# Where the sums of the last MLP's weight blocks are made: in SBUF at the time of use, or in DRAM during the first layer

## The chip, the cores and the metric

The kernel runs on one core of one Trainium2 chip. The metric is the device time of one execution in microseconds (us); three runs of the kernel before took 2469.17, 2469.54 and 2475.82 us, with a median of 2469.54 us. One more execution was profiled, and all rows below come from it.

## The reference

Two transformer-like layers are applied to 640 tokens: 128 context tokens and 512 latent tokens, which share all weights. All tensors are float32, with D_MODEL 1024 and D_FF 2816.

```python
def _layer(x, mod, p, lam_init, ctx_kv, rope):
    sh1, sc1, g1, sh2, sc2, g2 = jnp.split(mod, 6, axis=-1)
    h = _rmsnorm(x, p['norm1']) * (1 + sc1) + sh1
    ...   # three mixers on h @ p['w_in']: two attentions and a pooling mixer -> oa, ob, oc
    ga, gb, gc = jnp.split(jax.nn.sigmoid(h @ p['w_gate'] + p['b_gate']), 3, axis=-1)
    merged = ga * (oa @ p['w_br_a']) + gb * (ob @ p['w_br_b']) + gc * (oc @ p['w_br_c'])
    x = x + g1 * (merged @ p['w_out'])
    h2 = _rmsnorm(x, p['norm2']) * (1 + sc2) + sh2
    a, g = jnp.split(_dwconv3(h2 @ p['w_up'], p['conv_w'], p['conv_b']), 2, axis=-1)
    x = x + g2 * ((jax.nn.silu(a) * g) @ p['w_down'])
    return x, own_kv
```

`mod` is `silu(cond) @ w_mod + b_mod`, with `w_mod` of 1024 x 6144 for each layer. The change concerns `h2 @ p['w_up']` of the second (last) layer.

## The kernel before

Activations lie transposed: 128 channels on the partitions, 640 tokens in the free dimension. Every product keeps float32 accuracy by splitting both operands into a high and a low float32r part (`split`, L96 to L98: ScalarE copies the high part, VectorE subtracts for the low part) and running three matmuls (`mm3`, L115 to L117). A weight tile is 128 x 1024 floats: `load_w` (L100) takes a staging buffer `st` (3 of them), has SyncE (SP) issue the load (L104), and splits it into `wh` and `wl` (5 of each).

A layer runs through an attention phase, a merge phase (gates and branch projections, `merge_phase`), an output projection (`out_phase`) and the MLP. In the first layer the MLP goes through `mlp_up` (L860): 22 tile pairs f, each with one 128-channel tile of the part a and one of the part g; 48 matmuls go over each tile. Four groups of tile pairs (6, 6, 5, 5) are each followed by their share of the down projection (8 tiles each). `mod_steps` (L131) runs beside merge and MLP: it loads `w_mod` tiles of 512 KB and reduces them on VectorE. Its loads are paced (`paced`, L125): GpSimd (POOL) first copies one column from a tile that the compute has just made into the buffer, so that SP must wait for it.

The last layer's MLP (`mlp_last`, L1058) does the first three tile pairs in the plain way (`plain`, L916) and the other 19 with seven block products in place of eight (`SevenUp`). The weights of a tile pair are four blocks of 128 x 512, A(r, c), with r the part (a or g) and c the half of the 1024 inputs; the tokens are two halves of 320. The seven products need three plain blocks (`a11`, `a12`, `a22`) and four sums of blocks (`s1`, `s3`, `s2`, `s4`, with 2, 2, 3 and 4 terms). The token-side sums `n1`, `t2`, `n3`, `n4` are made once (`tokens`, L947). A call of `step` (L996) begins tile pair f and finishes the one before it, so the products of two pairs are interleaved; each product (`prod`, L991) is 12 matmuls. The three PSUM banks of a pair (`oa`, `od`, `ob`) are read by ScalarE and VectorE into `ua` and `ug` between the products (L1026 to L1048), and then go through the convolution and the gate (`conv`, `gated`).

`weights` (L969) loads two blocks into one tile. A sum is made in the staging buffer itself: SP loads its first term (L981), and POOL issues one accumulating DMA for every further term:

```python
                for m in range(1, 4):
                    for at, up in parts:
                        if m < len(up):
                            pool.dma_start(at, up[m], accum_op=ALU.add)
```

Each of these waits until the transfer before it into the same bytes has landed. Only then is the tile split and used. There are 133 loads and 133 accumulating transfers of 256 KB.

The order of instructions on each engine is set when the program is built, by a planner that simulates the program with its own costs and places instructions by priority; on the chip each engine, and each engine's DMA queue, runs its list in order. SP issues all plain DMAs in one list, POOL the accumulating ones between its other work.

Of the kernel before, what the change touches and what calls it, by code (L numbers as in the profile page):

```python
# [12 lines left out]
F32 = mybir.dt.float32  # L13
# [7 lines left out]
P = 128  # L21
# [5 lines left out]
L = 2  # L27
F_T = 22
EPS = 1e-6
GROUPS = [(0, 6), (6, 12), (12, 17), (17, 22)]  # L30
PLAIN = 3
WINDOWS = (2, 4, 8, 16)
FILL = [[], [('u', 3), ('u', 2), ('u', 1)], [('u', 0), ('g', 16)], [('g', 17), ('g', 18), ('p', 3), ('p', 2)], [('g', 19), ('p', 1), ('p', 0)], [('g', 20), ('g', 8)], [('g', 9), ('g', 10)]]
REST = [('g', 11)]
# [23 lines left out]
def trunk_kernel(ctx: ExitStack, tc: tile.TileContext, a: dict):  # L58
# [33 lines left out]
    g_dram = dram.tile([24, P, T], F32, name="g_dram")  # L92
    cs_dram = dram.tile([1, 2, 1024], F32, name="cs_dram")
    x_dram = dram.tile([P, ND, T], F32, name="x_dram")

    def split(x, hi, lo, eng=vec):  # L96
        act.activation(hi, x, AF.Copy)  # L97
        eng.tensor_tensor(out=lo, in0=x, in1=hi.bitcast(F32), op=ALU.subtract)  # L98

    def load_w(src, cols, eng=vec, after=None):  # L100
        st = wp.tile([P, 1024], F32, tag="st", name="st", bufs=3)
        if after is not None:
            pool.tensor_copy(st[:, 0:1], after)
        dma(st[:, :cols], src)  # L104
        hi = wp.tile([P, 1024], F32R, tag="wh", name="wh")
        lo = wp.tile([P, 1024], F32R, tag="wl", name="wl")
        split(st[:, :cols], hi[:, :cols], lo[:, :cols], eng)
        return hi, lo
# [22 lines left out]
    def mod_steps(l, groups, rp, cs, nst=3, npr=1, on_pool=()):  # L131

        for g in groups:
            got = small.tile([P, 8, 2], F32, tag="got", name="got")
            for m in range(8):
                st = rp.tile([P, 1024], F32, tag="stm", name="stm", bufs=nst)
                paced(st, a["w_mod"][l, 8 * g + m])
                for j in range(2):
                    col = got[:, m, j:j + 1]
                    if j == 0 and m in on_pool:  # L140
                        pr = rp.tile([P, 1024], F32, tag="pr", name="pr", bufs=npr)
                        pool.tensor_tensor(out=pr, in0=st, in1=cs[:, j], op=ALU.mult)
                        act.activation(pr, pr, AF.Copy, accum_out=col)
                    else:
                        junk = rp.tile([P, 1024], mybir.dt.bfloat16, tag="junk", name="junk", bufs=1)
                        vec.scalar_tensor_tensor(out=junk, in0=st, scalar=1.0, in1=cs[:, j], op0=ALU.mult,  # L146
                                                 op1=ALU.mult, accum_out=col)
                if m == 7:
                    bm = vecs[l][:, V_BM + 8 * g:V_BM + 8 * g + 8].unsqueeze(2).to_broadcast([P, 8, 2])
                    vec.tensor_tensor(out=mods[l][:, 8 * g:8 * g + 8], in0=got, in1=bm, op=ALU.add)  # L150
                yield

    def scale_cols(l, vcol, sc, name):
        t = small.tile([P, 8, 2], F32, tag=name, name=name, bufs=1)
# [592 lines left out]
            for _ in chain(flush(), *(run(j) for j in range(at, len(stream)))):  # L747
                pass

    def merge_phase(l, x, cs, hh, hl, mp, ps_d, msteps):  # L750

        m32 = [None] * 8
        for bi, br in enumerate((2, 1, 0)):
            oh = [None] * 4
            ol = [None] * 4

            def operands():
                for k in range(4):
                    oh[k] = mp.tile([P, T], F32R, tag="oh", name="oh", bufs=4)
                    ol[k] = mp.tile([P, T], F32R, tag="ol", name="ol", bufs=4)  # L760
                    st = mp.tile([P, T], F32, tag="so", name="so", bufs=3)
                    dma(st, o_dram[4 * br + k])
                    split(st, oh[k], ol[k])

            def gate(n, early0=False):
                gt = mp.tile([P, T], F32, tag="gt", name="gt", bufs=4)
                if br * 8 + n in GATED:
                    dma(gt, g_dram[br * 8 + n])
                    act.activation(gt, gt, AF.Sigmoid)
                    return gt  # L770
                gh, gl = load_w(a["w_gate"][l, br * 8 + n], 1024)
                gp = ps_d.tile("gp", bi > 0 or not early0)
                for k in range(ND):
                    ks = slice(k * P, (k + 1) * P)
                    for c, (a0, b0) in enumerate(CH_B):
                        mm3(gp[:, c, :320], gh[:, ks], gl[:, ks], hh[:, k, a0:b0], hl[:, k, a0:b0],
                            k == 0, k == 7)
                act.activation(gt.rearrange("p (c n) -> p c n", c=2), gp[:, :, :320], AF.Sigmoid,
                               bias=vecs[l][:, V_BG + br * 8 + n:V_BG + br * 8 + n + 1])
                return gt  # L780

            order = list(range(7, -1, -1) if br == 2 else range(8))
            wb, gts = None, {}
            for i, n in enumerate(order):
                for m in order[i:i + (LOOK if br == 2 and i == 0 else 2)]:
                    if m not in gts:
                        gts[m] = gate(m, i == 0)
                gt = gts[n]
                gv = gt.rearrange("p (c n) -> p c n", c=2)
                if i % 2 == 0:  # L790
                    wb = load_w(a["w_br"][l, br, n // 2], 1024)
                if i == 0:
                    operands()
                bp = ps_d.tile("bp")
                for k in range(4):
                    ks = slice(((n % 2) * 4 + k) * P, ((n % 2) * 4 + k + 1) * P)
                    for c, (a0, b0) in enumerate(CH_B):
                        mm3(bp[:, c, :320], wb[0][:, ks], wb[1][:, ks], oh[k][:, a0:b0], ol[k][:, a0:b0],
                            k == 0, k == 3)
                after[0] = gt[:, 0:1]  # L800
                if bi > 0:
                    if bi == 1:
                        if n == 0:
                            paced(cs[:, 0], cs_dram[:, 0].to_broadcast([P, 1024]))
                            paced(cs[:, 1], cs_dram[:, 1].to_broadcast([P, 1024]))
                        paced(x[:, n], (a["x"] if l == 0 else x_dram)[:, n])
                    if bi == 1 or n < 4:
                        next(msteps, None)
                        next(msteps, None)
                if bi == 0:  # L810
                    m32[n] = mp.tile([P, T], F32, tag="m32", name="m32", bufs=8)
                    vec.tensor_tensor(out=m32[n].rearrange("p (c n) -> p c n", c=2), in0=bp[:, :, :320], in1=gv,  # L812
                                      op=ALU.mult)
                else:
                    vec.tensor_tensor(out=gv, in0=bp[:, :, :320], in1=gv, op=ALU.mult)
                    (pool if bi == 1 else vec).tensor_tensor(out=m32[n], in0=m32[n], in1=gt, op=ALU.add)
# [68 lines left out]
    class SevenUp:  # L885
# [6 lines left out]


        BUFS = 7
        SUMS = {"a11": ((0, 0),), "a12": ((0, 1),), "a22": ((1, 1),), "s1": ((1, 0), (1, 1)), "s3": ((1, 0), (0, 0)),
                "s2": ((1, 0), (0, 0), (1, 1)), "s4": ((0, 1), (1, 0), (0, 0), (1, 1))}

        def __init__(self, l, h2h, h2l, mp, ps):
            self.l, self.h2h, self.h2l, self.mp, self.ps = l, h2h, h2l, mp, ps
# [69 lines left out]
        def weights(self, blocks):  # L969

            w = {}
            for i in range(0, len(blocks), 2):
# [1 line left out]
                st = wp.tile([P, 1024], F32, tag="st", name="st", bufs=3)  # L974
                hi = wp.tile([P, 1024], F32R, tag="wh", name="wh")
                lo = wp.tile([P, 1024], F32R, tag="wl", name="wl")
                parts = []
                for k, (q, f) in enumerate(two):
                    up = [a["w_up"][self.l, r * F_T + f, :, 512 * c:512 * c + 512] for r, c in self.SUMS[q]]
                    parts.append((st[:, k * 512:(k + 1) * 512], up))  # L980
                    dma(parts[-1][0], up[0])  # L981
                    w[q, f] = hi[:, k * 512:(k + 1) * 512], lo[:, k * 512:(k + 1) * 512]
                for m in range(1, 4):
                    for at, up in parts:
                        if m < len(up):
                            pool.dma_start(at, up[m], accum_op=ALU.add)  # L986
                n = 512 * len(two)
                split(st[:, :n], hi[:, :n], lo[:, :n])
                yield w
# [193 lines left out]
    a0, b0 = CH_S[2]  # L1183
    modulate(rp, x, rstd0(a0, b0), A1, mods[0][:, 0:8], a0, b0, hh[:, :, a0:b0], hl[:, :, a0:b0])
    sst.close()
    for l in range(L):
        dst.close()
        rst.close()
# [10 lines left out]
        with ExitStack() as ms:  # L1199
            mp = tp("mg", 1, ms)  # L1200
            cs = modp.tile([P, 2, 1024], F32, tag="cs", name="cs", bufs=1)
            msteps = mod_steps(l, range(2, 6 if l + 1 < L else 5), modp, cs)
            m32 = merge_phase(l, x, cs, hh, hl, mp, ps_d, msteps)
            hst.close()
            hst = ExitStack()
            hp = tp("h2p", 1, hst, side="right")
# [9 lines left out]
        with ExitStack() as ms:  # L1216
# [4 lines left out]
            def up_to(f):  # L1221
                for i in range(len(ups), f):
                    ups[i] = mlp_up(l, i, h2h, h2l, mp, ps_d)
                    for _ in range(1 if i < GROUPS[0][1] + 2 else 2):
                        next(msteps, None)

            for gi, (f0, f1) in enumerate(GROUPS):
                up_to(min(F_T, f1 + 2))
# [150 lines left out]
```

## Time and profile before

| | |
|---|---|
| runs | 2469.17, 2469.54, 2475.82 us |
| profiled execution | 2470.33 us, span 2468.6 us, mean granted TensorE clock 0.958 |
| busy share of the span | TensorE (PE) 90%, weight load 88%, VectorE (DVE) 67%, ScalarE (ACT) 42%, POOL 26% |
| HBM | read 282.91 MB, written 22.95 MB |
| layer 1: merge and out / MLP | about 390 to 690 / 690 to 1175 us |
| layer 2: attention / merge and out / MLP | about 1175 to 1550 / 1550 to 1819 / 1819 to 2468.6 us |

The span is the time from the first to the last instruction. Times in rows are us from its start unless marked ns. Matmuls overlap: one of 320 columns shows a duration near 310 ns, while the spacing is read from how many fit into a stretch. A row of waits says which engine and line waited, for which work, how long in total, how often, and the longest. A row of windows gives the busy us (and instructions) of PE, PEld (weight load), DVE, ACT and POOL in that order, then the granted TensorE clock as a share of 2.4 GHz, the busy share of the 16 DMA engines, and GB/s. Queue q0 is POOL's, which before holds little but the accumulating DMAs; q1 is SP's. L12 is line 12 of the kernel.

### The profile page before, as it was taken

How to read it: one execution, taken by the hardware profiler on the slowest of the kernel's cores; microseconds unless marked ns; L12 is line 12 of the kernel's file. 1: busy time of each engine (PE TensorE's matmuls, PEld its weight loads, DVE VectorE, ACT ScalarE, POOL GpSimd, SP SyncE). 2: the span in 40 equal slices, each digit the busy share in tenths (PEclk: the TensorE clock that was granted, in tenths of full speed). 3: DMA queues.
4: the chain of work that ended last, by engine and by line, in shares of the span. 5: the costliest groups of instructions: out<-in, count | busy, mean ns of one | idle time of the engine just before them, and what ended most of it. 6: DMA issues, size and time to landing. Idle time of an engine off the chain costs nothing. (4 is left out here: it accounts for less than half of the span.)

```text
span 2468.6 us, 38189 instructions
## 1 busy us (share of the span) xinstructions
PE 2233.9 (90%) x14550; PEld 2167.6 (88%) x14550; DVE 1644.7 (67%) x2983; ACT 1029.4 (42%) x1868; POOL 647.7 (26%) x784
## 2 busy tenths in 40 slices
PE   8998999999999999999898999999997786596868
PEld 4998989999999999999798989999996786596867
DVE  7876786496677576767877686489567535435536
ACT  5454654422454242434455565422345413313333
POOL 4753331051310000002653433042222112112120
PEclk8999999999999999999999999999998898798989
DMA  7212223574433334335121222375336666666665
GB/s 254 76 40 65 78 91 101 183 265 146 128 96 99 105 129 128 117 119 156 54 72 55 84 82 89 130 283 186 108 95 136 147 134 141 138 131 141 137 133 145
DMA packets 135611, 308.36 MB, mean 125 GB/s; under 512 B 23170, under 2 KB 36226, under 8 KB 135427
## 3 DMA queue, kind: packets, MB, share of 16 engines
q1 hardware_dynamic: 116276, 271.04, 33.8%
q0 software_dynamic: 19152, 34.87, 9.1%
q8 instruction: 115, 1.88, 0.3%
q14 instruction: 68, 0.56, 0.1%
HBM read 282.91 MB, written 22.95 MB: 124 GB/s over the span
## 5 line engine op out<-in xcount | busy, mean ns | idle before, releaser
L98 DVE TENSOR_TENSOR wl<-st,wh 128x1024 fp32r<-128x1024 f32 (+3 forms) x374 | 410.0, 1103 | 288.8 <-ACT wh L97 288.2
L97 ACT ACTIVATE wh<-st 128x1024 fp32r<-128x1024 f32 (+3 forms) x374 | 343.7, 931 | 483.8 <-DMA st<-in_w_up 211.2
L146 DVE SCALAR_TENSOR_TENSOR junk<-stm,cs 128x1024 bf16<-128x1024 f32 x172 | 220.3, 1281 | 56.1 <-DMA stm<-in_w_mod 53.4
L986 POOL DMA_DIRECT2D st<-in_w_up x133 | 116.1, 941 | 478.6 <-DMA st<-in_w_up 337.6
L116 PE MATMUL up<-h2l,wh 128*128 128x320 f32 x704 | 218.2, 311 | 1.3 <-DVE h2l L212 1.2
L115 PE MATMUL up<-h2h,wl 128*128 128x320 f32 x704 | 217.1, 311 | 1.2 <-ACT v L874 0.7
L117 PE MATMUL up<-h2h,wh 128*128 128x320 f32 x704 | 217.8, 310 | 0.0
L115 PE MATMUL mm<-wh,hl 128*128 128x384 f32 x480 | 170.8, 356 | 14.3 <-ACT raw L364 10.6
L116 PE MATMUL mm<-wl,hh 128*128 128x384 f32 x480 | 164.9, 343 | 1.3 <-DVE wl L98 1.3
L117 PE MATMUL mm<-wh,hh 128*128 128x384 f32 x480 | 164.5, 343 | 0.0
L117 PE MATMUL gp<-hh,wh 128*128 128x320 f32 x480 | 148.6, 310 | 0.0
L115 PE MATMUL gp<-hh,wl 128*128 128x320 f32 x480 | 148.4, 309 | 0.0
L116 PE MATMUL gp<-hl,wh 128*128 128x320 f32 x480 | 148.3, 309 | 0.0
L115 PE MATMUL mmu<-hh,wl 128*128 128x384 f32 (+1 forms) x416 | 133.5, 321 | 4.0 <-ACT up L680 2.0
L116 PEld LDWEIGHTS up<-h2l,wh 128*128 128x128 f32 x704 | 132.8, 189 | 1.8 <-DVE h2l L212 1.8
L115 PEld LDWEIGHTS up<-h2h,wl 128*128 128x128 f32 x704 | 132.3, 189 | 2.0 <-ACT h2h L211 1.1
L117 PEld LDWEIGHTS up<-h2h,wh 128*128 128x128 f32 x704 | 132.7, 189 | 0.1
L117 PE MATMUL mmu<-hh,wh 128*128 128x384 f32 (+1 forms) x416 | 130.5, 314 | 0.0
L116 PE MATMUL mmu<-hl,wh 128*128 128x384 f32 (+1 forms) x416 | 129.9, 312 | 0.0
L128 POOL COPY stm<-v 128x1 f32<-128x1 f32 x32 | 24.6, 792 | 381.7 <-DVE v L879 328.1
L115 PE MATMUL bp<-oh,wl 128*128 128x320 f32 x384 | 117.6, 311 | 3.6 <-DVE m L812 1.8
L116 PE MATMUL bp<-ol,wh 128*128 128x320 f32 x384 | 118.7, 310 | 2.1 <-DVE ol L98 2.1
(321 smaller groups left out, 6897.7 us busy)
## 6 DMA issues: line engine op xcount, KB each, us to landing
stm<-in_w_mod SPq DMA_DIRECT2D x88, 512.0 KB, 4.2
st<-in_w_up SPq DMA_DIRECT2D x133, 256.0 KB, 3.8
st<-in_w_up POOLq DMA_DIRECT2D x133, 256.0 KB, 5.6
st<-in_w_up SPq DMA_DIRECT2D x50, 512.0 KB, 3.6
st<-in_w_gate SPq DMA_DIRECT2D x48, 512.0 KB, 3.8
st<-in_w_unit SPq DMA_DIRECT2D x48, 384.0 KB, 3.3
st<-in_w_out SPq DMA_DIRECT2D x32, 512.0 KB, 3.5
st<-in_w_down SPq DMA_DIRECT2D x48, 320.0 KB, 3.2
```

Of the source, the lines that this page charges most:

```text
L97: act.activation(hi, x, AF.Copy)
L98: eng.tensor_tensor(out=lo, in0=x, in1=hi.bitcast(F32), op=ALU.subtract)
L115: pe.matmul(out, sl, mh, start=start, stop=False, skip_group_check=parts)
L116: pe.matmul(out, sh, ml, start=False, stop=False, skip_group_check=parts)
L117: pe.matmul(out, sh, mh, start=False, stop=stop, skip_group_check=parts)
L128: pool.tensor_copy(dst[:, 0:1], after[0])
L146: vec.scalar_tensor_tensor(out=junk, in0=st, scalar=1.0, in1=cs[:, j], op0=ALU.mult, op1=ALU.mult, accum_out=col)
L986: pool.dma_start(at, up[m], accum_op=ALU.add)
```

## The change

The four sums of each of the 19 tile pairs are made once, in a DRAM buffer `s_dram`, while the first layer runs. `sum_steps` is a generator with 22 steps. In step i SP issues four DRAM to DRAM copies of 256 KB for pair i (queued behind the latest weight load on SP's list), and POOL issues up to four accumulating DRAM to DRAM transfers: two for pair i-1 (s1 and s3, from `w_up`), one for pair i-2 (s2, adding the finished s1) and one for pair i-3 (s4, adding the finished s2). The steps are taken after each third tile of the merge phase (two per branch, six in all) and after four of five tile pairs of the first layer's MLP. In the last MLP all seven blocks are then plain loads by SP; `weights` issues nothing on POOL.

```diff
+    s_dram = dram.tile([F_T, 4, P, 512], F32, name="s_dram")
...
-        dma(st[:, :cols], src)
+        loads[:] = [dma(st[:, :cols], src)]
...
+    def sum_steps(l):
+        def A(r, c, f):
+            return a["w_up"][l, r * F_T + f, :, 512 * c:512 * c + 512]
+
+        def add(f, k, src):
+            if PLAIN <= f < F_T:
+                pool.dma_start(s_dram[f, k], src(f), accum_op=ALU.add, max_dma_last_dim=512)
+
+        for i in range(PLAIN, F_T + 3):
+            if i < F_T:
+                with tc.issue_after(loads[-1].ins):
+                    for k, (r, c) in enumerate(((1, 0), (1, 0), (0, 0), (0, 1))):
+                        dma(s_dram[i, k], A(r, c, i))
+            add(i - 1, 0, lambda f: A(1, 1, f))
+            add(i - 1, 1, lambda f: A(0, 0, f))
+            add(i - 2, 2, lambda f: s_dram[f, 0])
+            add(i - 3, 3, lambda f: s_dram[f, 2])
+            yield
...
+                if i % 3 == 2:
+                    next(ssteps, None)
...
-                parts = []
                 for k, (q, f) in enumerate(two):
-                    up = [a["w_up"][self.l, r * F_T + f, :, 512 * c:512 * c + 512] for r, c in self.SUMS[q]]
-                    parts.append((st[:, k * 512:(k + 1) * 512], up))
-                    dma(parts[-1][0], up[0])
+                    if q in self.PLACE:
+                        r, c = self.PLACE[q]
+                        src = a["w_up"][self.l, r * F_T + f, :, 512 * c:512 * c + 512]
+                    else:
+                        src = s_dram[f, SUMS.index(q)]
+                    dma(st[:, k * 512:(k + 1) * 512], src)
...
-                for m in range(1, 4):
-                    for at, up in parts:
-                        if m < len(up):
-                            pool.dma_start(at, up[m], accum_op=ALU.add)
...
+                    if i % 5 != 4:
+                        next(ssteps, None)
```

## Rows read from the trace of the kernel before

**Rows 1.** Windows: length, busy us (instructions) of five engines; PEclk, DMA share, GB/s.
```profile
690.00:1127.00 437.00, 433.53 (x2937) 431.70 (x2936) 300.42 (x527) 160.60 (x214) 27.38 (x36) 1.00 0.35 111
...
1700.00:1750.00 50.00, 50.00 (x343) 50.00 (x342) 31.70 (x45) 11.90 (x13) 1.82 (x4) 1.00 0.37 126
...
1870.00:1895.00 25.00, 7.01 (x32) 5.95 (x30) 14.61 (x19) 7.04 (x12) 4.75 (x6) 0.70 0.52 102
1895.00:1970.00 75.00, 57.47 (x343) 56.69 (x344) 46.76 (x67) 32.36 (x52) 14.39 (x17) 0.83 0.63 137
1970.00:2020.00 50.00, 47.34 (x322) 46.94 (x321) 24.41 (x41) 13.45 (x19) 9.59 (x11) 1.00 0.64 148
2020.00:2140.00 120.00, 75.59 (x429) 73.13 (x427) 54.48 (x74) 40.32 (x67) 26.12 (x30) 0.84 0.66 136
2140.00:2190.00 50.00, 42.50 (x272) 42.50 (x273) 24.88 (x39) 14.58 (x20) 6.11 (x7) 0.87 0.56 139
2190.00:2300.00 110.00, 75.68 (x438) 73.61 (x436) 48.25 (x68) 35.28 (x58) 25.28 (x29) 0.86 0.65 134
2300.00:2345.00 45.00, 41.46 (x272) 41.46 (x273) 23.96 (x41) 13.95 (x20) 6.08 (x7) 0.92 0.59 141
2345.00:2425.00 80.00, 49.44 (x289) 47.87 (x288) 35.98 (x51) 27.57 (x45) 15.70 (x18) 0.82 0.61 126
2425.00:2469.00 44.00, 38.72 (x259) 38.20 (x257) 26.78 (x48) 14.33 (x22) 0.00 (x0) 0.97 0.52 161
```

**Rows 2.** Waits of PE, 1819 to 2469 us.
```profile
PE ob L115 <- DVE wl L98: 82.4, 10, 11.0
PE od L115 <- DVE ua L1044: 21.8, 4, 9.6
PE od L115 <- DVE wl L98: 18.7, 7, 7.3
```

**Rows 3.** Waits of DVE and of ACT, 1819 to 2469 us.
```profile
DVE wl L98 <- ACT wh L97: 222.1, 64, 12.1
...
ACT wh L97 <- DMA st<-in_w_up: 211.2, 31, 14.9
```

**Rows 4.** Line L986, the accumulating DMAs: issue (min/median/max ns) and time to landing.
```profile
L986 POOL DMA_DIRECT2D st<-in_w_up x133: 862/865/1575, 1823.3 to 2416.7; - x133
...
DMA to landing us min/median/max: 3.7/5.6/9.0
```

**Rows 5.** Timeline of DVE, 1866 to 1900 us: start, duration, instruction, idle before.
```profile
1878.46 1.22 DVE L98 TENSOR_TENSOR wl<-st,wh 128x1024 fp32r<-128x1024 f32 x1 [11.00 <-ACT wh L97]
...
1884.82 3.02 DVE L960 TENSOR_TENSOR f<-h2h,h2l 128x640 f32<-128x640 f32 x4
```

**Rows 6.** DMA issues (part 6 of the page): count, KB each, median us to landing.
```profile
st<-in_w_up SPq DMA_DIRECT2D x133, 256.0 KB, 3.8
...
st<-in_w_up SPq DMA_DIRECT2D x50, 512.0 KB, 3.6
...
g_dram<-z SPq DMA_DIRECT2D x18, 320.0 KB, 2.2
gt<-g_dram SPq DMA_DIRECT2D x18, 320.0 KB, 3.9
```

**Rows 7.** DMA queues: packets, MB, share of 16 engines' span.
```profile
q1 hardware_dynamic: 116276, 271.04, 33.8%
q0 software_dynamic: 19152, 34.87, 9.1%
```

**Rows 8.** Window in the merge phase of layer 1, columns as in rows 1.
```profile
500.00:525.00 25.00, 25.00 (x172) 25.00 (x172) 24.60 (x32) 6.35 (x7) 15.22 (x13) 1.00 0.75 270
```

**Rows 9.** Waits of SP's queue and of POOL, 390 to 1130 us.
```profile
SPq L104 <- DVE wl L98: 338.2, 72, 27.2
SPq L129 <- POOL stm L128: 139.9, 49, 6.7
...
POOL stm L128 <- DVE v L879: 328.1, 17, 54.9
```

More of the change, by code (lines that the diff above doesn't have):

```diff
@@ L31 @@
 PLAIN = 3
+SUMS = ("s1", "s3", "s2", "s4")
 WINDOWS = (2, 4, 8, 16)
@@ L98, in split @@
         eng.tensor_tensor(out=lo, in0=x, in1=hi.bitcast(F32), op=ALU.subtract)
+    loads = []
     def load_w(src, cols, eng=vec, after=None):
@@ L748, in attention_phase, with merge_phase @@
                 pass
-    def merge_phase(l, x, cs, hh, hl, mp, ps_d, msteps):
+    def merge_phase(l, x, cs, hh, hl, mp, ps_d, msteps, ssteps):
         m32 = [None] * 8
@@ L894, in trunk_kernel @@
         BUFS = 7
-        SUMS = {"a11": ((0, 0),), "a12": ((0, 1),), "a22": ((1, 1),), "s1": ((1, 0), (1, 1)), "s3": ((1, 0), (0, 0)),
-                "s2": ((1, 0), (0, 0), (1, 1)), "s4": ((0, 1), (1, 0), (0, 0), (1, 1))}
+        PLACE = {"a11": (0, 0), "a12": (0, 1), "a22": (1, 1)}
         def __init__(self, l, h2h, h2l, mp, ps):
@@ L1185, in trunk_kernel @@
     sst.close()
+    ssteps = sum_steps(L - 1)
     for l in range(L):
@@ L1202, in trunk_kernel @@
             msteps = mod_steps(l, range(2, 6 if l + 1 < L else 5), modp, cs)
-            m32 = merge_phase(l, x, cs, hh, hl, mp, ps_d, msteps)
+            m32 = merge_phase(l, x, cs, hh, hl, mp, ps_d, msteps, ssteps)
             hst.close()
```

## The prediction, made before the changed kernel ran

> **What bounds the kernel now.** I first read the windows, stage by stage. In the first layer's MLP PE is busy 433.5 of 437 us, so that stage is bound by PE and hides its loads; a comparable stretch of the second layer's output projection, which like the seven products uses a weight tile for only 24 matmuls, holds 343 matmuls in 50.00 us, or 145.8 ns each [rows 1]. The last MLP is another matter. It has 3 x 96 plain matmuls, 19 x 7 x 12 = 1596 of the products and 3 x 8 x 2 x (6 + 6 + 5) + 240 = 1056 of the down projection. The four stretches in which the products run take 75 + 120 + 110 + 80 = 385 us [rows 1]. About 24 of the product matmuls lie before 1895 us, so these stretches do 1572, which at 145.8 ns is 229 us. They lose 156 us: PE is busy 57.5 + 75.6 + 75.7 + 49.4 = 258 us of them, so 127 us is idle, and the rest (258 - 229 = 29) is the granted clock of 0.82 to 0.86: part of the time at 1.2 in place of 2.4 GHz.
>
> Second I read who ended these waits. PE waits mostly for `wl`, the low half of a split weight tile (82.4 + 18.7 us), and 21.8 us for a VectorE operation on a bank [rows 2]. VectorE waits 222.1 us for the high half, and ScalarE, which makes it, 211.2 us for the DMA of the weights [rows 3]; so the releaser of the chain is a transfer, and a bank that is read late is partly VectorE stuck behind such a tile. Third, the line that issues the transfers: an accumulating DMA takes 0.865 us on POOL and lands a median 5.6 us after its issue [rows 4], and a tile needs up to three in a row after a load of 3.8 us [rows 6]: 3.8 + 3 x (0.9 + 5.6) = 23 us with three staging buffers, where the products want a tile per 24 x 0.1458 = 3.5 us. The DMA engines are 61 to 66% busy there [rows 1], so it is latency in a chain, with bandwidth left over, that limits the stage.
>
> **What the change removes.** All 133 accumulating DMAs leave the last MLP, and with them the chain. A tile then arrives 3.8 us after its load; adding the split (1.22 us on VectorE [rows 5], and ScalarE's part taken as long) gives about 6.2 us, against 3 x 3.5 = 10.5 us that three buffers allow. So weights should be on time.
>
> (1) Start of the products. VectorE stands 11.0 us in its list, until 1878.46, for the first late tile, and begins the token sums only at 1884.82 [rows 5]. PE has 7.0 us of work in the 25 us from 1870 to 1895 [rows 1]. The token sums stay, and so does PE's wait for them; the 11.0 us goes, of which I count 10. The products would run from 1885 us.
>
> (2) The products. What is late next? VectorE's busy time in the four stretches is 46.8 + 54.5 + 48.3 + 36.0 = 185.5 us over 1572 / 84 = 18.7 pairs, or 9.9 us a pair; ScalarE's 135.5 us, or 7.2; PE's 84 x 0.1458 = 12.25 us [rows 1]. PE is the bound, VectorE is at 81% of it and in order, and bank reads must fall between products. Lower end: PE with 3% loss, 236 us. Upper end: 15.5 us a pair, 290 us, the pace of the first stretch after its start (75 us for about 4.7 pairs is 16 [rows 1]), where the sums were no less late. I take 10% over the pure matmul time, 252 us: nearer to the output projection's row, which has the same need of weights and no loss, than to today's pace. That is 385 - 252 = 133 us less.
>
> (3) The down projections. 1056 matmuls are 154 us and take 50 + 50 + 45 + 44 = 189 us today; their losses are the clock (0.87 and 0.92 in two of the four) and waits at the seams with the products. The first stretch, at clock 1.00, holds 322 matmuls in 50 us, 6.5% over the pure time [rows 1]. With that everywhere, 164 us, and 4 us for the last additions and store: 168 us. Ends 160 and 185.
>
> So the last MLP ends at 1885 + 252 + 168 = 2305 in place of 2468.6 us.
>
> **What it adds to the first layer.** 76 copies and 76 adds of 256 KB, DRAM to DRAM, a kind that this trace doesn't show. POOL: 76 x 0.865 = 66 us of issuing, at most four (3.5 us) at a step; POOL is busy 27.4 of 437 us in that MLP [rows 1] and spends 328.1 us waiting for a VectorE result before its pacing copies [rows 9]. DMA engines: SP's queue moved 271.04 MB in 33.8% of 2468.6 us, 325 GB/s while busy; POOL's 34.87 MB in 9.1%, 155 GB/s [rows 7]. The copies' 19.9 MB then take 61 us of engine time (128 at POOL's rate), the adds' 128 us; the lower bound for the adds is 61 us, the upper one is one transfer at a time, 76 x 5.6 = 426 us [rows 4]. In the MLP stretch 13 groups of copies and 59 adds fall, 42 + 100 us, beside 0.35 x 437 = 153 us of today's traffic [rows 1]: 295 of 437, a share of 0.68, which fits. In the merge phase the share is already 0.75 and VectorE is busy 24.6 of 25 us [rows 8]; a step adds about 3 + 7 = 10 us of engine time where some 6 of 25 us is free, so loads get late by some us at about three steps. SP normally waits for free buffers there (338.2 us [rows 9]), so loads run ahead, and most of this is hidden. I take 8 us of lost PE time in the first layer, with ends -3 (no row shows anything that could be gained but PE's idle 3.5 us) and +35 (adds at half of POOL's rate: 295 becomes 395 of 437, and every merge step late). The cover is the prefetch: three staged and five split tiles, each good for 48 matmuls or 7 us. SP's copies wait for nothing; POOL's adds wait for copies or adds of the step before, at least 14 us old (96 matmuls). Queued behind a waiting add are POOL's pacing copies, for which SP waits (139.9 us in 49 waits today, 6.7 at most [rows 9]), and behind them the weight loads.
>
> Span 2305 + 8 = 2313. The profiled execution took 2470.33 us for 2468.6 of span, 1.7 more, and stands 0.8 above the median of the runs: **2315 us**, 6.3% less.
>
> **Rivals.**
> A. The products stay late for another reason: VectorE's order, or a bank read that comes too late, takes the place of the transfers, and each stall costs some us at the 1.2 GHz level as now. For it: VectorE at 81% of PE's time, 21.8 us of PE's waits on `ua` [rows 2]. Against: VectorE itself waited 222.1 us for weights [rows 3]. At 15.5 us a pair and 180 us of down projections: 2315 + 38 + 12 = 2365.
> B. PE runs through, as in the output projection: products 236, downs 160 us, first layer nothing: 2315 - 16 - 8 - 8 = 2283, and 2275 if the tokens come earlier too.
> C. Slower than before: the adds saturate the DMA engines in the first layer, and the weight loads there get late, where PE has nothing to spare. For that the last MLP's 164 us must be lost again. 437 + 164 = 601 us of engine time, less 153 and 42, leaves 406 us for 59 adds (15.5 MB): the point is at 38 GB/s, a quarter of POOL's rate [rows 7]; at 35 GB/s the time would be 2507. Against: the two ends of an add are memory, and of the two single sides the trace shows that 320 KB written to DRAM lands in 2.2 us while the same read takes 3.9 [rows 6], so a write isn't the slow side. The Trainium skill ("DMA: Bandwidth & Descriptors", section on the anatomy of one DMA on the SWDGE path) says the opposite, that completion waits for the write's receipt and takes surprisingly long when the target is HBM; by it the adds would land later than 5.6 us and hold POOL's list, by the rows no later, and in either case the wait is for a transfer issued a step earlier. The same page (section "Issuing engines are not separate DMA queues") has POOL's and SP's transfers share the same engines; the trace agrees: beside the accumulates a 256 KB load takes 3.8 us, elsewhere 512 KB takes 3.6 [rows 6]. That is what keeps C alive.
> D. The change doesn't do what it says: reads of the sums wait for the adds, because the adds lag. The last step is taken in the MLP's pair 18 of 22, so before 1127 us [rows 1], and the first sums are read near 1820 [rows 4]; a lag of 700 us is out of reach. Under 1%, time as before.
>
> **Chances.** The forecast, 2285 to 2335: 55%. A, 2335 to 2400: 24%. B, below 2285: 14%. Between 2400 and 2460 (A and half of C together): 3%. C: 3%; D and other ways to no change: 1%. Leaving out about 2 in 10, the range is 2275 to 2380. A run can be told from no change at about 0.3% (7 us): faster 0.95, same 0.01, slower 0.04.
>
> **What the changed profile would show.** Waits of ScalarE for the DMA of `w_up` in the last MLP near 20 to 40 us in place of 211; no accumulating DMA after 1175 us, and POOL nearly idle there; token sums beginning within a few us of 1874; windows of products with 270 or more matmuls in 50 us and a clock over 0.95. In the first layer: PE still over 430 of 437 us, with a DMA share near 0.65; if it is 0.9 or over and PE has waits for `wl`, the engine-time sum is wrong and C's mechanism is at work. If adds land in over 15 us, POOL's rate doesn't hold between two places in memory. The prediction is wrong in its main step if the product stretches shrink by less than 90 us while the weights come on time; then it is VectorE's order that was under it.

## The result, and the profile after

The changed kernel took 2332.14 us (median of 4 runs, 2327.22 to 2334.83) against 2471.29 us for the kernel before in the same comparison; the ratio is 0.9432, with a 95% interval from 0.9409 to 0.9456. The prediction was 2315 us. Its profiled execution took 2327.22 us, with a span of 2325.4 us. The total hides two moves in opposite directions. The last output-projection matmul of the second layer, after which the last MLP runs, started at 1868.5 us where it had been at 1818.8; from there to the end it was 649.8 us before and is 456.9 now. So the last MLP gained 193 us, and all that comes ahead of it lost 50.

The last MLP first. Windows of the kernel after, columns as in [rows 1]: token sums, a stretch of products, the first down projection, the next products, and all from the first product with token sums on.
```profile
1915.00:1932.00 17.00, 7.47 (x51) 7.21 (x50) 12.95 (x17) 5.82 (x11) 0.00 (x0) 0.80 0.25 80
1932.00:1985.00 53.00, 51.37 (x332) 50.97 (x333) 48.17 (x69) 34.34 (x55) 0.00 (x0) 0.93 0.41 119
1985.00:2036.00 51.00, 51.00 (x350) 51.00 (x349) 27.94 (x45) 15.74 (x22) 0.00 (x0) 1.00 0.29 93
2036.00:2115.00 79.00, 79.00 (x540) 79.00 (x539) 66.75 (x95) 49.90 (x82) 0.00 (x0) 1.00 0.45 139
...
1932.00:2318.00 386.00, 382.88 (x2585) 381.99 (x2586) 283.47 (x425) 195.70 (x306) 0.00 (x0) 0.99 0.40 122
```
PE is busy 382.9 of 386 us at a granted clock of 0.99 (2.4 GHz nearly throughout). The second stretch of products, 429 matmuls in 120 us before [rows 1], now holds 540 in 79.00 us without a gap: 146.3 ns each, where the output projection's stretch had 145.8. (The bounds of the stretches are drawn by hand, so they don't hold the same matmuls.) The waits of [rows 2] and [rows 3], for the kernel after from 1819 to 2330 us, which takes in the 50 us ahead of the last MLP (PE, VectorE, ScalarE):
```profile
PE od L119 <- ACT n L99: 9.9, 1, 9.9
PE oa L119 <- DVE wl L100: 1.5, 1, 1.5
```
```profile
DVE wl L100 <- ACT wh L99: 40.8, 58, 5.1
```
```profile
ACT wh L99 <- PE ob L121: 66.9, 44, 4.7
...
ACT wh L99 <- DMA st<-in_w_down: 9.9, 5, 4.0
```
Here the direction has turned round: ScalarE's splits wait for PE to give buffers back, not for `w_up` to arrive: no wait for it is left. PE's one long wait is for the token sums.

Now the first layer. The same stretch as the first row of [rows 1], and the waits of POOL, SP, VectorE and PE from 390 to 1180 us:
```profile
690.00:1127.00 437.00, 401.94 (x2646) 397.59 (x2645) 282.09 (x494) 148.96 (x204) 81.19 (x86) 0.96 0.65 163
```
```profile
POOL s_dram L166 <- DMA s_dram<-in_w_up: 204.8, 32, 21.2
...
POOL s_dram L166 <- DMA s_dram<-s_dram: 80.1, 17, 8.5
```
```profile
SPq L133 <- POOL stm L132: 183.3, 42, 15.7
```
```profile
DVE junk L150 <- DMA stm<-in_w_mod: 97.5, 23, 12.2
```
```profile
PE up L119 <- ACT v L902: 17.4, 5, 7.7
```
The last two of these, in the kernel before:
```profile
DVE junk L146 <- DMA stm<-in_w_mod: 40.4, 20, 3.3
```
```profile
PE up L115 <- ACT v L874: 0.7, 1, 0.7
```
PE holds 291 matmuls fewer in the 437 us, which is 42 us of work at 145.8 ns: 31.6 us of busy time are gone, and the rest goes with a granted clock of 0.96 in place of 1.00. POOL stands 284.9 us in front of its adds (L166). The other three rows are the links by which that reaches PE. One instance can be followed in the timelines of the kernel after, POOL, SP, VectorE, ScalarE and PE, 800 to 830 us (start, duration, engine, instruction, idle time before it and its releaser):
```profile
801.88 1.06 POOL L166 DMA_DIRECT2D s_dram<-s_dram  x1 [3.69 <-DMA s_dram<-in_w_up]
807.39 1.01 POOL L166 DMA_DIRECT2D s_dram<-s_dram  x1 [4.46 <-DMA s_dram<-s_dram]
808.04 0.56 POOL L132 COPY stm<-v 128x1 f32<-128x1 f32 x1
```
```profile
808.62 0.33 SPq L133 DMA_DIRECT2D stm<-in_w_mod  x1
```
```profile
813.38 1.23 DVE L150 SCALAR_TENSOR_TENSOR junk<-stm,cs 128x1024 bf16<-128x1024 f32 x1 [9.79 <-DMA stm<-in_w_mod]
```
```profile
819.57 0.74 ACT L881 ACTIVATE v<-v 128x640 f32<-128x640 f32 x1 [12.89 <-DVE v L907]
```
```profile
821.73 0.63 PE L119 MATMUL up<-h2h,wl 128*128 128x320 f32 x1 [7.70 <-ACT v L902]
```
The add of s4 waits for the landing of s2; the pacing copy stands behind it on POOL's list; SP issues the `w_mod` load as the copy ends (0.6 us after its start); VectorE has this reduction next on its list and stands 9.8 us; the convolution and the SiLU come late; ScalarE empties the PSUM bank late; PE waits 7.7 us for the bank. PE has no wait for a weight tile anywhere from 390 to 1180 us; its second longest, 9.5 us in all, is for VectorE's additions of the down projection.

### The profile page after: what moved, and what is told of

Its sections match the earlier page's. It is cut to its first block, busy times and chain, and to the rows that moved or that the text cites. A ratio compares the mean times of both kernels' runs of the same rounds, so it can differ in the third digit from the quotient of the medians.

```text
span 2325.4 us, 38200 instructions
## 1 busy us (share of the span) xinstructions
PE 2198.9 (95%) x14550; PEld 2136.6 (92%) x14550; DVE 1646.5 (71%) x2983; ACT 1030.9 (44%) x1868; POOL 607.5 (26%) x727
## 3 DMA queue, kind: packets, MB, share of 16 engines
q0 software_dynamic: 40128, 19.93, 7.3%
## 5 line engine op out<-in xcount | busy, mean ns | idle before, releaser
L121 PE MATMUL bp<-oh,wh 128*128 128x320 f32 x384 | 119.1, 312 | 0.0
L485 DVE TENSOR_TENSOR pl<-pt,ph 128x512 fp32r<-128x512 f32 (+2 forms) x156 | 89.6, 580 | 38.5 <-ACT ph L484 18.6
```

Of the source, the lines that this page charges most:

```text
L121: pe.matmul(out, sh, mh, start=False, stop=stop, skip_group_check=parts)
L485: vec.tensor_tensor(out=pl[:, :n], in0=ps[:, :n], in1=ph[:, :n].bitcast(F32), op=ALU.subtract)
```

## The experiments

Each median stands beside runs of the kernel before on the same chip, with medians of 2468 to 2473 us, and the ratio is to these; the changed kernel wasn't run again beside them, so versions are best compared by their ratios (0.9432 for the changed kernel). The two theories on the first layer's 50 us were: T1, the bytes (the DMA engines are too busy, loads get late); T2, POOL's list (adds that wait hold the pacing copies).

**Only the reads.** No sums are made:
```diff
-    ssteps = sum_steps(L - 1)
+    ssteps = iter(())
...
-                        src = s_dram[f, SUMS.index(q)]
+                        src = a["w_up"][self.l, f, :, :512]
```


> The four sums aren't made at all: the last MLP reads plain blocks of w_up in their place (the seven products then use wrong operands), and the first layer has no copies and no adds. It shows the gain of the last MLP without what the sums cost. In the changed kernel the last MLP took 193 us less than before (649.6 to 456.7) and the first layer 51.6 us more, so both theories expect 2332 - 51 = 2281 us (2274 to 2290). If it stays above 2310, the first layer's longer time isn't the price of the sums.


Measured 2282.28 us (ratio 0.9234, 0.9213 to 0.9254). The sums cost 50 us, all of it ahead of the last MLP, which took 456.5 us here and 456.9 in the changed kernel. This is also the floor: what the time would be if the sums cost nothing.

**Only the copies.**
```diff
-                pool.dma_start(s_dram[f, k], src(f), accum_op=ALU.add, max_dma_last_dim=512)
+                pass
```


> The 76 adds on POOL are left out (each sum keeps its first term only); the 76 copies on SP stay. Theory T1 (the DMA engines are full, and the first layer's loads get late by the amount of traffic): the copies are about a third of the added engine time, so about a third of the loss of 51 us stays: 2298 (2292 to 2310). Theory T2 (adds that wait for a transfer hold POOL's list, and behind them the pacing copies for which SP and then VectorE wait): nothing waits on POOL, so the first layer is within 8 us of before: 2281 to 2289.


Measured 2283.21 us (0.924, 0.9218 to 0.9262): SP's 76 copies cost nothing that can be told (the first layer's last matmul on `w_up` starts at 1130.9 us in this run and in the one before it). T1's 2298 is missed. The price is in the adds, as T2 has it, but their bytes are in the adds too.

**A longer lag in the code.**
```diff
-            add(i - 1, 0, lambda f: A(1, 1, f))
-            add(i - 1, 1, lambda f: A(0, 0, f))
-            add(i - 2, 2, lambda f: s_dram[f, 0])
-            add(i - 3, 3, lambda f: s_dram[f, 2])
+            add(i - 2, 0, lambda f: A(1, 1, f))
+            add(i - 2, 1, lambda f: A(0, 0, f))
+            add(i - 4, 2, lambda f: s_dram[f, 0])
+            add(i - 6, 3, lambda f: s_dram[f, 2])
```
(The loop has three steps more, and the first layer's MLP takes them.)


> The same copies and adds with the same bytes, but each add is issued twice as many steps after what it needs (2, 2, 4 and 6 steps after the copy in place of 1, 1, 2 and 3; 25 steps in place of 22). T1: traffic is unchanged, so the time is too: 2332 (2324 to 2340), with VectorE's waits for w_mod near 97 us in the first layer. T2: POOL's waits of 285 us for transfers shrink to under 60, and the first layer loses under 20 us: 2285 to 2300.


Measured 2334.9 us (0.9449, 0.9424 to 0.9474). T2's number failed and T1's fits. But POOL's waits for transfers were still 281.6 us (199.2 + 82.4), so the lag had not done what it was to do, and the run doesn't speak on T2.

**Pacing copies on VectorE.**
```diff
-            pool.tensor_copy(dst[:, 0:1], after[0])
+            vec.tensor_copy(dst[:, 0:1], after[0])
```


> The pacing copies (one column, before each w_mod, x and cs load) are made by VectorE in place of POOL; copies and adds are as in the changed kernel. T1: 2332 (2324 to 2340). T2: POOL may wait as before, but SP's paced loads no longer stand behind it; what stays is the rstd power and the additions on POOL (some 10 us at the head of the first MLP): 2290 to 2310, with VectorE's waits for w_mod in the first layer back to about 40 us from 97.


Measured 2298.42 us (0.9301, 0.9283 to 0.932). The same adds, the same bytes, 34 us of the 50 gone, while POOL waits even longer (373.5 us). POOL and VectorE, 390 to 1180 us:
```profile
POOL s_dram L166 <- DMA s_dram<-in_w_up: 285.0, 31, 53.1
...
POOL s_dram L166 <- DMA s_dram<-s_dram: 88.5, 16, 10.4
```
```profile
DVE junk L150 <- DMA stm<-in_w_mod: 45.9, 24, 4.9
```
That is against T1, and it shows the link: a waiting POOL costs little once nothing that SP needs stands behind it. It is still 16 us above the floor; the expectation put some 10 of them down to other work on POOL, which no run shows.

**Why the lag did nothing: a buffer per pair.** The longer lag again, with separate, separately named DRAM buffers:
```diff
-    s_dram = dram.tile([F_T, 4, P, 512], F32, name="s_dram")
+    s_dram = [dram.tile([4, P, 512], F32, name="s_dram" + "defghijklmnopqrstuvwxyz"[f]) for f in range(F_T)]
```
(The places that use `s_dram` are indexed to match.)


> The longer lag of the run before it, with a DRAM buffer of its own (its own name) for every tile pair. The longer lag left POOL's waits as they were (282 us). Theory T3 (adds of different pairs wait for each other because they share one buffer): separate buffers take these waits away, under 60 us of them stay and the time is 2285 to 2300. Theory T2b (the planner undoes the lag: on POOL's list the four adds of one pair stand in a row, and s2 waits for its own s1, s4 for its own s2, each a landing of 5 us): the waits stay near 280 us, the names in POOL's timeline show rows of one pair, and the time is 2328 to 2342.


Measured 2329.89 us (two runs; 0.9425, 0.9406 to 0.9444), with 283 us of waits. The names tell what POOL does, 880 to 960 us:
```profile
889.72 2.55 POOL L166 DMA_DIRECT2D s_dramu<-in_w_up  x2 [7.53 <-DMA s_dramu<-in_w_up]
896.04 1.05 POOL L166 DMA_DIRECT2D s_dramu<-s_dramu  x1 [3.77 <-DMA s_dramu<-in_w_up]
904.32 1.01 POOL L166 DMA_DIRECT2D s_dramu<-s_dramu  x1 [7.22 <-DMA s_dramu<-s_dramu]
904.96 2.95 POOL L166 DMA_DIRECT2D s_dramv<-in_w_up  x2
911.59 1.05 POOL L166 DMA_DIRECT2D s_dramv<-s_dramv  x1 [3.67 <-DMA s_dramv<-in_w_up]
916.39 1.02 POOL L166 DMA_DIRECT2D s_dramv<-s_dramv  x1 [3.75 <-DMA s_dramv<-s_dramv]
917.04 0.68 POOL L132 COPY stm<-v 128x1 f32<-128x1 f32 x2
```
All four adds of pair u stand in a row, then those of pair v: s2 waits for its own s1, s4 for its own s2, and the pacing copies come after both pairs. The code had them steps apart; the planner, which is free to move them, had gathered them. It wasn't the shared buffer (T3). In the changed kernel the names can't tell pairs apart, but POOL's list has the same pattern there: two adds from `w_up`, a wait of 3.2 us, one from `s_dram`, a wait of 8.0 us, one more (886.80 to 901.64 us).

**Adds tied behind the pacing copies.** `paced` keeps its last copy in `paces`, and
```diff
-                pool.dma_start(s_dram[f, k], src(f), accum_op=ALU.add, max_dma_last_dim=512)
+                with tc.issue_after(paces[-1].ins) if paces else ExitStack():
+                    pool.dma_start(s_dram[f, k], src(f), accum_op=ALU.add, max_dma_last_dim=512)
```


> The changed kernel with its own lags, but each add is tied on POOL's list behind the pacing copy that was issued last before its step, so that the planner can't gather the adds of a pair; copies, adds and bytes are the same. T2b: an add then waits for what landed a step earlier; POOL's waits for transfers in the first layer fall from 285 to under 80 us, VectorE's for w_mod from 97 to near 40, and the time to 2283 to 2300. T1 (traffic): 2324 to 2340.


Measured 2286.6 us (0.9253, 0.9234 to 0.9271). POOL waits, and its timeline at the same place:
```profile
POOL s_dram L168 <- DMA s_dram<-in_w_up: 20.3, 1, 20.3
```
```profile
917.49 2.55 POOL L168 DMA_DIRECT2D s_dram<-in_w_up  x2
919.02 3.15 POOL L168 DMA_DIRECT2D s_dram<-s_dram  x2
931.58 1.35 POOL L133 COPY stm<-v 128x1 f32<-128x1 f32 x2 [9.42 <-DVE v L909]
```
Four adds in one go after a pacing copy, none waiting for a transfer; of 284.9 us of waits one of 20.3 is left, in the merge phase, ahead of the first pacing copy. VectorE's wait for `w_mod` is 56.6 us, not quite the 40 that was expected. Issued four at a time the adds land later than before, 8.9 us (from `w_up`) and 11.2 us (from `s_dram`) in place of 6.5 and 5.0, but nothing stands behind them. The time is within 5 us of the floor, with every byte still moved: the waits, not the bytes, were the price. This version beats both kernels.

**Larger packets, alone and with the tie.** `max_dma_last_dim=2048` in place of 512:


> Only the limit on the last dimension of the adds is changed, 2048 in place of 512. POOL's queue moved 19.93 MB in 40128 packets, 497 bytes each; with 2 KB packets it should be near 10000. T1: the adds' share of the DMA engines (7.3% of the span, 117 GB/s) falls to that of the accumulating DMAs before (155 GB/s) and with it about a quarter of their loss: 2315 to 2325. T2b: a wait is a landing, mostly latency; POOL's issue gets shorter (1.3 to about 0.9 us) and waits shrink a little: 2318 to 2332.

> Both edits together: adds tied behind the pacing copies and 2 KB packets. If traffic still costs something once the waits are gone, this is faster than the tied adds alone, by 3 to 8 us: 2280 to 2292. If waits were all, the two are within 3 us of each other. Floor: the run with neither copies nor adds, 2282.


Alone 2319.0 us (0.9379, 0.9363 to 0.9396), 13 us better: both theories allowed that, and POOL's waits hardly moved (277.7 us), so which part of the smaller packets or of the shorter issue (0.81 us at the median, in place of 1.30 from `w_up` and 1.06 from `s_dram`) gave it is not settled. The landing hardly changed (6.4 and 5.2 us), which speaks for the issue. With the tie 2288.05 us (0.9256, 0.9241 to 0.9272), the same as the tie alone: once nothing waits, packets cost nothing here.

**The tie with the longer lag.**


> The adds tied behind the pacing copies, and the longer lag (2, 2, 4 and 6 steps) on top. In the run with tied adds alone the first layer's MLP still ended 12 us later than with neither copies nor adds (up stage 1142.9 against 1130.9 us). If what is left there is waiting, the longer lag takes it: 2279 to 2286. If it is the transfers' share of the DMA engines or the merge phase, where the adds ahead of the first pacing copy can't be tied: 2284 to 2292, no change.


Measured 2285.54 us (0.9259, 0.924 to 0.9277): equal to the tie alone within the intervals. The first layer's up stage ends at 1135.1 us in place of 1143.0 (1130.9 in the run without sums), but the medians can't tell the two.

**Was the last MLP bound by latency or by bandwidth?** Two tries to put its 133 transfers back as bytes on which nobody waits. `TERMS` lists the further terms of each sum, `scr` holds 133 scratch buffers in DRAM.
```diff
+                    for r, c in TERMS.get(q, ()):
+                        dma(scr.pop(), a["w_up"][self.l, r * F_T + f, :, 512 * c:512 * c + 512])
```


> The changed kernel, with the 133 transfers that left the last MLP put back as bytes alone: for each further term of a sum SP also copies that block of w_up to a scratch buffer in DRAM, on which nobody waits. Theory L (before, the last MLP was bound by the latency of a chain of dependent transfers): the bytes alone cost little; the last MLP stays within 15 us of its 457 us and the whole at 2332 to 2347. Theory B (it was bound by what the DMA engines could move, at a busy share of 0.61 to 0.66): with the share back at 0.6 or over the last MLP goes back by at least half of its 193 us, and the whole to over 2425.


Measured 2362.75 us (0.9572, 0.9545 to 0.9599), and the run missed its question: the copies were issued between 28.4 and 158.7 us, at the start of the program, and cost 31 us there, with the DMA engines at a share of 0.98 to 1.00 for 165 us; the last MLP had none. The second try ties them on SP's list:
```diff
-                    dma(st[:, k * 512:(k + 1) * 512], src)
+                    ld = dma(st[:, k * 512:(k + 1) * 512], src)
+                    with tc.issue_after(ld.ins):
+                        for r, c in TERMS.get(q, ()):
+                            dma(scr.pop(), a["w_up"][self.l, r * F_T + f, :, 512 * c:512 * c + 512])
```


> The same question again, since the planner had moved all 133 scratch copies of the run before to the first 160 us of the program. Now each is tied on SP's list behind the load of its own sum, so that the bytes move in the last MLP; nobody waits for them, but loads stand behind up to three of them in SP's queue. Theory L (latency of dependent transfers bound the stage before): last MLP within 15 us of 457 us with a DMA share of 0.6 or over, the whole 2332 to 2347. Theory B (bandwidth at a share of 0.61 to 0.66): the last MLP goes back by at least half of its 193 us, the whole to over 2425.


Measured 2333.1 us (0.9432, 0.9411 to 0.9452), the time of the changed kernel, with a last MLP of 457.7 us. The scratch copies, and the window that answers to 1932 to 2318 above:
```profile
L1015 SPq DMA_DIRECT2D scr<-in_w_up x133: 490/497/1731, 1875.3 to 2272.2; - x133
```
```profile
1940.00:2325.00 385.00, 382.25 (x2585) 381.35 (x2586) 283.98 (x426) 194.77 (x305) 0.00 (x0) 0.99 0.64 202
```
The DMA share is 0.64, as before the change, at 202 in place of 126 to 148 GB/s, and PE still is busy 382 of 385 us. The stage was bound by waiting for one transfer after another, not by what the DMA engines can move. These bytes are plain copies, not accumulating transfers; that those cost little too when nobody waits for them is shown by the tied adds, in the first layer only.

## Why the prediction was right, and where it was not

**What bounds the kernel: right.** Theory B, bandwidth, fell with the tied scratch copies.

**(1) The start: right.** From the last output-projection matmul to the first product with token sums it was 1893.1 - 1818.8 = 74.3 us and is 1932.4 - 1868.5 = 63.9: 10.4 us less, where 10 were forecast. The token sums began 55.6 us after that matmul in place of 66.0, and PE's wait of 9.9 us for them stayed.

**(2) and (3) Products and down projections: the mechanism right, the loss too large.** 420 us were forecast from the first such product to the end; it took 2325.4 - 1932.4 = 393. I had allowed 10% over the pure matmul time for VectorE's order and 6.5% for the down projections; in the window the 2585 matmuls at 145.8 ns are 377 of 386 us, a loss of 2.4%, of which 0.8% is idle time. So the term that was too large is the allowance for stalls. Rival B was right for this part: with VectorE at 283.5 of 386 us, in order, PE runs through, as in the output projection of [rows 1]. The 6.5% was read from a stretch (1970 to 2020 us) that itself still suffered from a late tile: PE's only wait there is for an addition that stood on VectorE's list behind the split of one.
```profile
2009.41 1.22 DVE L98 TENSOR_TENSOR wl<-st,wh 128x1024 fp32r<-128x1024 f32 x1 [8.03 <-ACT wh L97]
```
```profile
PE od L115 <- DVE x L1054: 2.7, 1, 2.7
```
Two readings in this part of the prediction were off, without harm to its sum. The four stretches of products hold 1499 matmuls by [rows 1], not 1572, and those of the down projections 1125, not 1056: only the split between the two was wrong. And 343 matmuls in the first stretch are 4.1 pairs, not 4.7, so its pace was 18 us a pair, and the upper end of 15.5 (rival A's too) wasn't that pace.

**The first layer: wrong, and the step that failed was the one that called the adds' waits covered.** The text had "POOL's adds wait for copies or adds of the step before, at least 14 us old". That is the order in the code. On POOL's list the planner had put the four adds of a pair in a row, where they wait for each other; the cost was 50 us, against 8 with an upper end of 35. In the profiled executions 48 of them show between the run without sums and the changed kernel at the last matmul on `w_up` (1130.9 and 1179.3 us), 6 of the 48 ahead of the first one (693.6 and 699.6 us). The chain behind it (pacing copies behind the adds, SP behind the copies, weight loads behind SP) stood in the same paragraph, but with no price, because the lag was taken for granted. Only its last link was other than said: not the weight loads but the `w_mod` loads came late, and VectorE, in order, carried the delay to PE through a PSUM bank. For most of the 6 us ahead of the MLP another link shows: PE's one long wait in the merge phase, 7.2 us, is for an attention output that was loaded late (ScalarE waited 29.2 us for these loads, 10.0 with the tied adds).

**The engine time: right.** A share of 0.68 was forecast for that MLP; it was 0.65, and the copies alone cost nothing. Adds landed in 6.5 us (from `w_up`) and 5.0 (from `s_dram`), as the accumulating DMAs into SBUF had in [rows 4]. 320 KB written from SBUF to DRAM landed in 2.2 us, and plain copies of 256 KB from DRAM to DRAM in 5.7 us (5.2 in the last MLP with the scratch copies), where loads of that size into SBUF took 2.8 to 4.0 us. The Trainium skill ("DMA: Bandwidth & Descriptors", section on the anatomy of one DMA on the SWDGE path), weighed under rival C, has a target in HBM delay completion most. These rows don't settle that rule: the adds show no clear surcharge, the copies took longer than loads, and a write alone was fast.

Transfers do slow each other: loads of 256 KB of `w_up` in the last MLP land in 2.8 us, where they took 3.8 beside the accumulating ones [rows 6] and 3.5 beside the scratch copies. The Trainium skill ("DMA: Bandwidth & Descriptors", section "Issuing engines are not separate DMA queues") says that transfers started by different engines run on the same DMA engines and interleave; the traces agree. But sharing engines cost the first layer little at a share of 0.65 to 0.71 (the changed kernel and the tied adds); sharing POOL's list cost it most.

**The signs.** POOL idle in the last MLP and the DMA share in the first came as said. ScalarE's wait for `w_up` in the last MLP vanished, where 20 to 40 us were said, and the first stretch of products had a clock of 0.93, where over 0.95 was said. PE in the first layer's MLP fell to 401.9 us, where over 430 was said; as it came without waits for `wl` and with a share of 0.65, C's own signs were absent.

In sum, 2315 with 42 us more for the first layer and 27 less for the last MLP is 2330, beside a profiled 2327.2. The errors partly cancelled, and it is partly luck that the time fell inside 2285 to 2335: with the loss in the first layer alone put right the sum would be 2357. Rival C's direction, time lost in the first layer, was real at about a third of its size and by another mechanism than full DMA engines.

## What to carry to other kernels

Where idle engine time is due to a chain of dependent transfers, taking the chain away can give nearly all of it back even at the same bytes (here PE was left idle for 0.8% of the 386 us); check with transfers on which nobody waits. A wait in an in-order list is priced by what stands behind it there, and where a planner writes the list, steps that the code puts apart may stand side by side: read the list, or tie the instructions. When a change moves work to a stage that was full, look there for the part of the gain that is missing.

## What the runs showed that was not expected

- Copies of 256 KB from DRAM to DRAM on SP's queue landed in 5.7 us, against 2.9 for the load of a sum into SBUF, and 76 of them cost the first layer nothing measurable (2283.21 against 2282.28 us). The 133 scratch copies cost 31 us where they filled the DMA engines (a share of 0.98 to 1.00) and nothing at 0.64.
- With the limit of 512 the adds moved in packets of 497 bytes on average (19.93 MB in 40128), with 2048 in packets of 1821 bytes (10944); POOL's queue then took 5.8% of 2313.2 us in place of 7.3% of 2325.4, 149 against 117 GB/s.
- Four adds issued without a wait between them took POOL 4.7 us in the run with the tie (917.49 to 922.17 us), about 1.2 us an issue.
